# A small store of 444-byte rows moved from among the last loads to behind them

## The chip, the cores and the metric

The kernel runs on one core of one Trainium2 chip. The metric is device time in microseconds (us) of one execution. Lower is better. The executions of this kernel agree within about 0.3%.

## The reference

The input is x of 32 x 512 x 1024 float32. Negative values become zero, and the last axis is summed:

```python
def reference(x):
    relu_x = np.maximum(x, 0)
    return np.sum(relu_x, axis=-1).astype(np.float32)
```

That is 67.11 MB to read and 64 KB to write.

## The kernel before

SP issues every transfer in program order. Seven large pieces of x go through three buffers. Then comes a tail of ever smaller loads, down to three pieces of one last row per partition (512, 224 and 288 columns). ACT and DVE share the compute. The 128 results of a partition leave in three stores: 128 results that were transposed first (four runs of 128 bytes, "the four-run store"), 111 results per partition (128 rows of 444 bytes, "the 444-byte store"), and the 16 results of the tail (64 bytes per partition, "the last store"). SP's end of the program, shortened:

```python
    # ... tail loads: rows of 8, 4, 2, 1 per partition, then the last row in three pieces
    for k, (lo, hi) in enumerate([(0, n0), (n0, n1), (n1, D)]):
        sp.dma_start(out=parts[k], in_=xv[-1][:, BIG - 1, lo:hi]).then_inc(
            s_in[NBIG + len(TAIL) + k] if k < 2 else s_part, 16
        )
    sp.wait_ge(s_fact, 1)          # the last results of the 444-byte store are there
    sp.wait_ge(s_fdve, 1)
    sp.dma_start(out=ov[1][:, :], in_=res[:, start[1] : start[2]]).then_inc(s_store, 16)
    sp.wait_ge(s_turn, 1)
    sp.dma_start(
        out=of[0:P].rearrange("(k q) -> k q", q=32), in_=turned[0:P:32, 0:32]
    ).then_inc(s_store, 16)
    # ...
    sp.wait_ge(s_tdve, 1)          # the very last result
    sp.dma_start(out=ov[-1][:, :], in_=res[:, start[-1] : J]).then_inc(s_out, 16)
    sp.wait_ge(s_store, 16 * (len(REGIONS) - 1))
    sp.wait_ge(s_out, 16)
```

The compute of the last row matters too. Note that one semaphore, `s_part`, counts the last load (16) and the two engines (1 each):

```python
    act.wait_ge(s_in[-2], 16)
    on_act(parts[0], last[:, n : n + 1]).then_inc(s_part, 1)
    dve.wait_ge(s_in[-1], 16)
    on_dve(parts[1], last[:, n + 1 : n + 2]).then_inc(s_part, 1)
    dve.wait_ge(s_part, 16 + 2)
    on_dve(last[:, :], res[:, J - 1 : J]).then_inc(s_tdve, 1)
```

## Time and profile before

| | before |
|---|---|
| median of 3 runs | 161.09 us (160.91 to 161.38) |
| profiled execution | 161.31 us, span 160.0 us |
| DVE, ACT busy | 76%, 63% of the span |
| DMA queue of SP | 97.8% of 16 engines' span, 420 GB/s |
| chain that ended last | loads 68%, ACT 18%, DVE 11%, SP 1% |

The kernel is bound by its loads, and after them by a short end of compute and one store. A number of the chain is the share of the span in which that piece of work was what the end waited for.

### The profile page before, as it was taken

To read this page: it belongs to the slowest core of one execution; us is meant where nothing else is said; L and a number is where in the kernel's file an instruction comes from. 1 tells how busy PE (TensorE), PEld (TensorE's weight loads), DVE (VectorE), ACT (ScalarE), POOL (GpSimd) and SP (SyncE) were. 2 spreads that over 40 slices of the span, in tenths; PEclk is the share of its full clock that TensorE was granted. 3 is DMA by queue.
4 is the path that set the end of the run, shared out by engine and by line. 5 is a ranking of instruction groups with operands and counts; after the bars stand their busy time and mean duration, and the time that the engine had idled before them with its cause. 6 is when DMAs were issued, how large, how long until landed. Compare 5 with 4: busy or idle time off the path is not lost.

```text
span 160.0 us, 150 instructions
## 1 busy us (share of the span) xinstructions
DVE 121.6 (76%) x59; ACT 101.4 (63%) x55; POOL 0.2 (0%) x4
## 2 busy tenths in 40 slices
DVE  0000000999959999999979989699899999598994
ACT  3000059990799708996099942999339980596973
POOL 0000000000000000000000000000000000000000
DMA  9997996996996997997998979969969969999993
GB/s 377 492 399 338 492 524 262 524 524 262 524 508 279 524 475 311 524 442 344 524 410 377 524 344 443 524 295 492 524 295 492 524 262 524 393 393 406 418 387 119
DMA packets 2457, 67.18 MB, mean 420 GB/s; under 512 B 536, under 2 KB 792, under 8 KB 1176
## 3 DMA queue, kind: packets, MB, share of 16 engines
q1 hardware_dynamic: 2456, 67.18, 97.8%
q14 instruction: 1, 0.01, 0.0%
HBM read 67.11 MB, written 0.07 MB: 420 GB/s over the span
## 4 chain that ended last, share of the span: by engine, by line
DMA 68%; ACT 18%; DVE 11%; SPq 1%; issue 0%
DMA buf<-in_x_dram 68%; ACT buf L137 18%; DVE res L152 11%; ACT buf L119 1%; SPq L98 1%; DVE last L122 0%
## 5 line engine op out<-in xcount | busy, mean ns | idle before, releaser
L152 DVE TENSOR_REDUCE res<-buf 128x7 f32<-128x7168 f32 (+4 forms) x17 | 100.1, 5920 | 33.6 <-ACT buf L137 33.6
L137 ACT ACTIVATE buf<-buf 128x7168 f32<-128x7168 f32 (+4 forms) x16 | 80.7, 5099 | 45.9 <-DMA buf<-in_x_dram 45.9
L119 ACT ACTIVATE buf<-buf 128x1024 f32<-128x1024 f32 (+1 forms) x19 | 19.0, 1001 | 9.2 <-DMA buf<-in_x_dram 9.2
L122 DVE TENSOR_SCALAR_CACHE_REDUCE buf<-buf 128x1024 f32<-128x1024 f32 (+2 forms) x19 | 20.8, 1144 | 2.9 <-DMA buf<-in_x_dram 2.7
L119 ACT ACTIVATION_READ_ACCUMULATOR buf<-buf 128x1 f32 x19 | 3.6, 187 | 0.0
L137 ACT ACT_TABLE_LOAD x1 | 1.3, 1283 | 1.3 <-PEq L215 1.3
L122 DVE DVE_READ_ACCUMULATOR buf<-buf 128x1 f32 x19 | 1.6, 82 | 0.0
L122 DVE TENSOR_SCALAR_CACHE_REDUCE last<-last 128x290 f32<-128x290 f32 x1 | 0.5, 455 | 0.2 <-ACT buf L119 0.2
L161 DVE STREAM_TRANSPOSE turned<-res 128x32 f32<-128x32 f32 x1 | 0.2, 211 | 0.0
L185 DVE TENSOR_TENSOR res<-half 128x1 f32<-128x1 f32 x1 | 0.2, 160 | 0.1
L215 POOL MEMSET const-bfloat16-1.0<- 128x1 bf16 x1 | 0.1, 101 | 0.0
L215 POOL MEMSET const-uint8-127<- 128x1 uint8 x1 | 0.1, 101 | 0.0
L215 POOL MEMSET const-float32-0.0<- 128x1 f32 x1 | 0.1, 98 | 0.2 <-issue 0.2
L215 POOL MEMSET const-float32-1.0<- 128x1 f32 x1 | 0.1, 98 | 0.0
L122 DVE DVE_READ_ACCUMULATOR last<-last 128x1 f32 x1 | 0.1, 82 | 0.0
## 6 DMA issues: line engine op xcount, KB each, us to landing
buf<-in_x_dram SPq DMA_DIRECT2D x1, 7680.0 KB, 21.3
buf<-in_x_dram SPq DMA_DIRECT2D x1, 4096.0 KB, 26.7
buf<-in_x_dram SPq DMA_DIRECT2D x1, 2048.0 KB, 31.2
buf<-in_x_dram SPq DMA_DIRECT2D x2, 512.0 KB, 18.8
buf<-in_x_dram SPq DMA_DIRECT2D x1, 1024.0 KB, 33.2
buf<-in_x_dram SPq DMA_DIRECT2D x1, 256.0 KB, 34.4
last<-in_x_dram SPq DMA_DIRECT2D x1, 144.0 KB, 34.3
buf<-in_x_dram SPq DMA_DIRECT2D x1, 112.0 KB, 34.1
```

Source lines behind the costliest of these rows:

```text
L98: sp.dma_start(out=buf[:, tb, r : r + n, :], in_=xv[-1][:, r : r + n, :]).then_inc(s_in[NBIG + i], 16)
L119: return act.activation(t, t, AF.Relu, accum_out=acc)
L122: return dve.tensor_scalar(out=t, in0=t, scalar1=0.0, scalar2=None, op0=ALU.max, op1=ALU.add, accum_out=acc)
L137: act.activation(t, t, AF.Relu).then_inc(s_act, 1)
L152: dve.tensor_reduce(out=res[:, c * BIG + r : c * BIG + r + n], in_=buf[:, c % NB, r : r + n, :], axis=X, op=ALU.add,).then_inc(s_dve, 1)
L161: dve.transpose(out=turned[:, :], in_=res[:, 0:32]).then_inc(s_turn, 1)
L185: dve.tensor_tensor(out=res[:, j0 + r : j0 + r + 1], in0=half[:, 0:1], in1=half[:, 1:2], op=ALU.add)
L215: nc = _bacc.Bacc("TRN2", target_bir_lowering=False, num_devices=1)
```

## The change

The intent: the small writes of the 444-byte store are suspected of disturbing the loads beside which they run, so that store waits until the last load but one has landed. The four-run store, which takes SP longest to issue (0.63 us), goes ahead of it so that it is out of the way.

```diff
-    sp.wait_ge(s_fact, 1)
-    sp.wait_ge(s_fdve, 1)
-    sp.dma_start(out=ov[1][:, :], in_=res[:, start[1] : start[2]]).then_inc(s_store, 16)
     sp.wait_ge(s_turn, 1)
     sp.dma_start(
         out=of[0:P].rearrange("(k q) -> k q", q=32), in_=turned[0:P:32, 0:32]
     ).then_inc(s_store, 16)
+    sp.wait_ge(s_fact, 1)
+    sp.wait_ge(s_fdve, 1)
+    sp.wait_ge(s_in[-1], 16)
+    sp.dma_start(out=ov[1][:, :], in_=res[:, start[1] : start[2]]).then_inc(s_store, 16)
```

## The prediction

> **What bounds the kernel now.** I began with the page's chain of work that ended last, because the change touches only the last microseconds of the program and only what is on that chain there can move the time.
>
> ```profile
> DMA 68%; ACT 18%; DVE 11%; SPq 1%; issue 0%
> DMA buf<-in_x_dram 68%; ACT buf L137 18%; DVE res L152 11%; ACT buf L119 1%; SPq L98 1%; DVE last L122 0%
> ```
>
> No store stands on it. The loads of x carry 68% of the span; the rest is two earlier rounds of compute that release buffers, the issue of the tail loads, and a short end. The chain in order of time shows that end (start, duration, what):
>
> ```profile
> 122.21 34.19 DMA buf<-in_x_dram
> 156.40 0.02 issue
> 156.42 1.56 ACT buf L119 x4
> 157.98 0.02 issue
> 158.00 0.46 DVE last L122 x2
> ```
>
> The reader is to see where the chain leaves the loads: at 156.40, with the landing of the last whole row (the load issued at 122.21). From there ACT is the bound, with half of that row and then half of the last row back to back, 1.56 us, then one DVE instruction, 0.46 us, and then the last store. Loads that land after 156.40 (the three pieces of the last row) do not set the end: ACT is not idle between its two pieces, and the DVE's last instruction waits for ACT, not for a DMA:
>
> ```profile
> 157.08 0.63 ACT L119 ACTIVATE buf<-buf 128x512 f32<-128x512 f32 x1
> 158.00 0.46 DVE L122 TENSOR_SCALAR_CACHE_REDUCE last<-last 128x290 f32<-128x290 f32 x1 [0.24 <-ACT buf L119]
> ```
>
> Next I asked for SP's own order of issues, since SP issues every transfer of this kernel in program order:
>
> ```profile
> 147.17 0.35 SPq L111 DMA_DIRECT2D out_dram<-res  x1
> 147.56 0.63 SPq L113 DMA_DIRECT2D out_dram<-turned  x1
> 158.49 0.34 SPq L199 DMA_DIRECT2D out_dram<-res  x1
> ```
>
> L111 is the store of 128 rows of 444 bytes (111 results per partition), L113 the four-run store, L199 the last store (16 results, 64 bytes, per partition). The first two go out at 147, when ten microseconds of loads are still to come. It looks as if they disturb those loads. The stretches of the tail say otherwise (columns: stretch, length, DVE, ACT and POOL busy, clock, DMA share, GB/s):
>
> ```profile
> 146.50:156.25 9.75, 8.82 (x16) 7.61 (x14) 0.00 (x0) 1.00 0.98 401
> 156.25:156.75 0.50, 0.33 (x1) 0.33 (x1) 0.00 (x0) 1.00 1.05 369
> 156.75:157.25 0.50, 0.44 (x3) 0.50 (x3) 0.00 (x0) 1.00 0.91 289
> 157.25:157.50 0.25, 0.21 (x2) 0.25 (x1) 0.00 (x0) 1.00 0.18 49
> 157.50:159.25 1.75, 0.73 (x4) 0.30 (x2) 0.00 (x0) 1.00 0.00 0
> 159.25:159.50 0.25, 0.00 (x0) 0.00 (x0) 0.00 (x0) 1.00 0.36 32
> ```
>
> Two things are to be seen: the engines are full until 156.75 and then run empty, and from 157.50 until the last store starts at about 159.3 they do nothing at all, a hole of 1.75 us. The packets of the trace by size say whose these are: the first 444-byte packet starts at 156.84 and the last ends at 157.54, although their store was issued at 147.17. They waited 9.7 us behind the loads. The last pieces' load packets run until 157.36, so 0.5 us of the store lies beside the end of the loads, on engines that have finished their own.
>
> **What the Trainium skill says.** (1) "DMA: Bandwidth & Descriptors", section "Queues, rings and completion order": on each DMA engine the descriptors of one issuing queue are consumed in ring order. The trace agrees: issued at 147.17, first packet 156.84, when the first engine runs out of loads. (2) The same page, "Specifications": below 512 bytes a transfer does a read-modify-write, so 444-byte rows are presumably what made the author suspicious. The trace shows 25 ns for a 444-byte packet against 41 ns for 896 bytes and 51 ns for 1,152, that is 56, 46 and 44 ps per byte: a quarter dearer per byte, not a multiple. (3) "Perfetto Trace Analysis", section "DMA Instruction — HWDGE (DVE, Sync)": the final semaphore write waits for the data to be written, which can take surprisingly long towards HBM. This trace shows no such delay for these stores: the last 64-byte packet starts at 159.52, the last semaphore write 159.53, and the execution ends at 160.0.
>
> **The change, part by part.** The instructions and their number are the same on every engine; the listing of SP's order shows two DMA issues swapped and one wait added (for the 224-column piece, the last load but one).
>
> (a) *The four-run store moves ahead.* It waits only for the transpose after the second round, long done when SP has issued its loads at 123.69 + 0.44 = 124.1. It is then issued at about 124.2 instead of 147.56. SP has nothing else to do there (the next wait is for the compute until 147.17), so its 0.63 us is free. Its four packets took 13 ns each; still issued after all loads, they still queue behind them. Effect on the path: 0.
>
> (b) *The 444-byte store stays away from the loads.* It moves from 147.17 to the landing of the 224-column piece. The last 896-byte packet ends at 156.98, its last semaphore write at about 157.00, so issue at about 157.05. The last store gives the time from issue to first packet: 158.49 to 159.33, 0.84 us. So packets from 157.9. Each engine has 128/16 = 8 rows, at some 21 to 25 ns each 0.2 us (the trace shows them spaced 21 ns): done by about 158.1. This is inside the idle hole from 157.50 to 159.3.
>
> (c) *What is gained.* The most the store could have cost the loads is its own engine time, 128 x 25 ns / 16 engines = 0.2 us, 0.12% of the time, and only if it lay ahead of them. It did not. On the engines that finish last, the 1,152-byte packets are spaced 47 ns while the store runs beside them and 47 ns before it began: no slowing to recover. And the chain left the loads at 156.40, before the first 444-byte packet at 156.84. Gain on the path: 0.0 us.
>
> (d) *What is lost.* SP is busy with this issue from 157.05 to 157.40 and must be free at 158.49 for the last store: 1.1 us to spare. If the wait ended only when the DVE took up the piece, at 157.37, SP would be free at 157.72 and the packets done by 158.5: still before 159.3. The last two waits of the program (stores done) see the earlier store done at least 0.8 us before the last one. Loss on the path: 0.0 us.
>
> Sum: 0.0. From the median of 161.09, and with the slight leaning towards a gain that a quieter end of the loads might have, I say 161.05.
>
> **The rivals.** *First, contention:* the small writes slow the last loads, by sharing memory rather than an engine, and taking them away brings landings forward. For it: in 156.75 to 157.25 the rate falls to 289 GB/s while the DMA share is 0.91. Against it: short packets alone explain that, the packet spacing did not change, and only landings after 156.40 could profit, for which nobody on the chain waits. Even granting all 0.2 us the time would be 160.9. *Second, a new late completion:* the 444-byte store is now so late that its completion ends the program, or its issue holds up the last store on SP. For it: the distance falls from 1.8 us (157.54 to 159.33) to about 1.2 us, and a write receipt of some 2 us, which the skill's delay in (3) would allow, would end near 160. Against it: no receipt shows in this trace. It would make 161.3 to 161.6. *Third, the early four-run store gets in front:* if its packets at 124 ran at once, they would cost four packets of 13 ns among loads, nothing that can be measured. *Fourth, the last store starts later*, because descriptors of the 444-byte store still fill its queue: it would need them to be unfinished at 159.3, 1.2 us later than computed; if so, 161.3.
>
> **Range and chances.** The three runs of before span 160.91 to 161.38, 0.3%. My effect is between -0.2 (first rival in full) and +0.4 (second rival), most likely within 0.05 of nothing, so the scatter of the runs sets the range: 160.70 to 161.45. A gain of over 2% would need 3.2 us; the whole end after the loads' leg of the chain is 160.0 - 156.4 = 3.6 us and the change removes none of it. A loss of 2% would need the store to finish at about 163. I give 0.01 to faster, 0.98 to within 2%, 0.01 to slower.
>
> **What would show each step right or wrong.** Right: the four-run store's issue near 124.2; the 444-byte store's issue between 157.0 and 157.4; packets under 512 bytes gone from 157.0 to 157.4 but for semaphore writes, and a burst near 157.9 to 158.2 in the former hole; the chain still leaving the loads near 156.4, ACT 1.56 us, DVE 0.46 us and the last store's issue 2.1 us after the loads' leg; no store on the chain but the last. Wrong: a chain whose last load leg ends more than 0.1 us earlier relative to the start of the tail loads (contention was real), a final issue that follows another SP issue directly, or a span that ends with the 444-byte store's landing. A shift of the whole program by some tenths, with the end from 156.4 on unchanged, would be scatter and say nothing of the change.

## More of the kernel before

The three calls of experiments ran on three chips (7, 15 and 2, four kernels each), so times are compared within a call. All runs told of are with a granted clock of 1.00. Where "the trace's records" are named, they are the packet and semaphore records from which the profile is made.

## The result

| | median | runs | range |
|---|---|---|---|
| before | 161.06 us | 6 | 160.91 to 161.38 |
| changed | 160.98 us | 6 | 160.84 to 161.12 |

The ratio is 0.9993, with a 95% interval of 0.998 to 1.0006: the same. Ratios are the mean time of one kernel's runs over that of the other's of the same rounds, so they are not quite the ratio of the medians quoted.

SP's issues in the changed kernel, in order of time (start, duration, line, what):

```profile
123.50 0.44 SPq L106 DMA_DIRECT2D last<-in_x_dram  x1
123.99 0.63 SPq L110 DMA_DIRECT2D out_dram<-turned  x1
157.16 0.34 SPq L116 DMA_DIRECT2D out_dram<-res  x1
158.05 0.34 SPq L200 DMA_DIRECT2D out_dram<-res  x1
```

The four-run store goes out at 123.99, directly behind the loads, and the 444-byte store at 157.16, as predicted. The packets of the 444-byte store are now in the hole that the DMA engines had near the end. The stretches of the changed kernel (columns as in the prediction: stretch, length, DVE, ACT and POOL busy, clock, DMA share, GB/s):

```profile
157.25:157.50 0.25, 0.23 (x2) 0.25 (x2) 0.00 (x0) 1.00 0.00 0
157.50:157.75 0.25, 0.19 (x1) 0.03 (x1) 0.00 (x0) 1.00 0.00 0
157.75:158.50 0.75, 0.27 (x2) 0.00 (x0) 0.00 (x0) 1.00 0.27 76
158.50:158.75 0.25, 0.00 (x0) 0.00 (x0) 0.00 (x0) 1.00 0.00 0
158.75:159.25 0.50, 0.00 (x0) 0.00 (x0) 0.00 (x0) 1.00 0.19 17
```

The work of 157.75 to 158.50 is the 444-byte store (the trace's records: first packet 158.00, last 158.32), and the last store follows from 158.88.

The chain that ended last, in the changed kernel, in order of time:

```profile
122.06 34.02 DMA buf<-in_x_dram
156.09 0.02 issue
156.11 1.43 ACT buf L120 x4
157.53 0.02 issue
157.56 0.46 DVE last L123 x2
```

It has the same pieces as before, but the load's leg is 0.17 us shorter than before (34.19) and ACT's leg 0.13 us shorter (1.56), although ACT has the same four instructions with the same durations. I had not predicted the second. With another 0.14 us from the start of the tail loads, which lies before the change takes effect and so is scatter, this makes up the 0.44 us by which the two profiled spans differ (159.953 and 159.510 in the trace's records). The medians, however, differ by 0.08 us only. Either the profiled execution of before was unlucky, or it shows something that most executions hide. That question set the experiments.

The shorter ACT leg has this explanation in the trace's semaphore records. The DVE's last instruction waits for `s_part` to reach 18. Before, ACT's increment came at 157.81, but the last of the sixteen increments of the last load came at 157.98, and the instruction began at 158.00. In the changed kernel the load's last came at 157.40, ACT's at 157.53, and the DVE began at 157.56. So the line that my prediction quoted, "0.24 <-ACT buf L119", named the wrong releaser. One semaphore with several writers does not tell the profile who came last.

### The profile page after: what moved, and what is told of

The parts are those of the page before. It is cut to its first block, busy times and chain, and to the rows that moved or that the text cites. A ratio compares the mean times of both kernels' runs of the same rounds, so it can differ in the third digit from the quotient of the medians. Undisturbed runs are those within 1.5% of the kernel's fastest.

```text
span 159.5 us, 150 instructions
## 1 busy us (share of the span) xinstructions
DVE 121.6 (76%) x59; ACT 101.5 (64%) x55; POOL 0.2 (0%) x4
## 4 chain that ended last, share of the span: by engine, by line
DMA 68%; ACT 18%; DVE 11%; SPq 1%; issue 0%
DMA buf<-in_x_dram 68%; ACT buf L138 18%; DVE res L153 11%; ACT buf L120 1%; SPq L98 1%; DVE last L123 0%
```

## The experiments

Twelve kernels ran. Theory Q is my prediction's: the early store queues behind the loads and takes nothing from the path. Its rivals grew with the results; each theory is explained in the expectation that first names it. All results were correct but that of the kernel that leaves a store out on purpose. "Completion lag" is, by the trace's records, the time from the end of the last packet of the last load (1,152-byte packets) to the last of that load's sixteen semaphore increments. "Gap" is from ACT's end to the start of the DVE's last instruction.

| kernel | median us (range) | before, same call | ratio (95% interval) | profiled us | completion lag | gap |
|---|---|---|---|---|---|---|
| before (first profile) | 161.09 | | | 161.31 | 0.62 | 0.20 |
| changed | 160.98 (160.84 to 161.12) | 161.06 | 0.9993 (0.998 to 1.0006) | 160.86 | 0.45 | 0.03 |
| e_after_again | 160.90 (160.85 to 161.02) | 160.94 | 0.9998 (0.9985 to 1.0012) | 160.85 | 0.45 | 0.03 |
| e_no_store | 160.90 (160.86 to 160.99) | 160.94 | 0.9997 (0.9985 to 1.001) | 160.90 | 0.45 | 0.03 |
| e_early_x8 | 163.24 (163.10 to 163.50) | 160.94 | 1.0144 (1.013 to 1.0157) | 163.12 | 0.31 | 0.03 |
| e_wait_only | 162.19 (162.08 to 162.34) | 160.94 | 1.0076 (1.0063 to 1.0088) | 162.21 | 0.45 | 0.03 |
| e_before_again | 161.14 (160.98 to 161.48) | 161.05 | 1.0006 (0.9992 to 1.002) | 161.48 | 1.07 | 0.54 |
| e_split_before | 161.07 (160.96 to 161.42) | 161.05 | 1.0001 (0.9988 to 1.0013) | 161.11 | 0.62 | 0.13 |
| e_late_four | 161.10 (160.87 to 161.37) | 161.05 | 1.0000 (0.9987 to 1.0013) | 161.26 | 0.66 | 0.13 |
| e_just_before_last | 162.28 (162.24 to 162.34) | 161.05 | 1.0073 (1.006 to 1.0086) | 162.34 | 0.43 | 0.03 |
| e_swap_only | 161.14 (160.97 to 161.47) | 160.96 | 1.0011 (0.9998 to 1.0023) | 161.47 | 1.07 | 0.52 |
| e_split_after | 160.98 (160.91 to 161.12) | 160.96 | 1.0002 (0.999 to 1.0015) | 161.12 | 0.47 | 0.13 |
| e_act_queue | 161.24 (160.97 to 161.44) | 160.96 | 1.0022 (1.0008 to 1.0036) | 160.97 | 0.45 | 0.03 |
| e_wait_last | 161.25 (160.97 to 161.41) | 160.96 | 1.0014 (1.0002 to 1.0027) | 161.41 | 0.45 | 0.13 |

### e_after_again: the changed kernel once more

No edit. 

> The changed kernel again, beside the kernel before on one chip, to narrow the interval. Theory Q (the early store queues behind the loads and takes nothing from the path): ratio 1.000, within 0.0005 of it, 161.06 us. Rival C (the store's packets hold up the completion of the last load, whose last semaphore increment came at 157.98 in the trace before, 0.17 us after ACT's; in the trace after ACT was last by 0.14 us): 0.1 to 0.2 us faster, ratio 0.9988 to 0.9994.

It came out at 160.90 beside 160.94. The effect, 0.04 us, is nearer to Q than to C, and zero effect (a ratio of 1) is within the interval. The profile repeats the first one's: lag 0.45, gap 0.03.

### e_no_store: what the store costs at all

Against the changed kernel:

```diff
-    sp.wait_ge(s_fact, 1)
-    sp.wait_ge(s_fdve, 1)
-    sp.wait_ge(s_in[-1], 16)
-    sp.dma_start(out=ov[1][:, :], in_=res[:, start[1] : start[2]]).then_inc(s_store, 16)
...
-    sp.wait_ge(s_store, 16 * (len(REGIONS) - 1))
+    sp.wait_ge(s_store, 16)
```

> The changed kernel with the 444-byte store left out (14,208 results are not written: the result is wrong on purpose). It shows all that this store can cost wherever it stands. Theory Q: as the changed kernel and as the kernel before, within 0.1 us. Rival C: as the changed kernel, and 0.1 to 0.2 us faster than before. Rival L (the late store costs something at the end): faster than the changed kernel by 0.1 us or more.

160.90 us, just as the changed kernel's 160.90 of the same call. In the changed kernel the store is hidden as far as these runs can tell, so Rival L is out. Against the kernel before, all that could be gained is of the order of 0.05 us in the median.

### e_early_x8: the early store eight times over

```diff
     sp.dma_start(out=ov[1][:, :], in_=res[:, start[1] : start[2]]).then_inc(s_store, 16)
+    for i in range(7):
+        sp.dma_start(out=spare[i], in_=res[:, start[1] : start[2]]).then_inc(s_store, 16)
```

(with `spare` an internal tensor in HBM, and the last wait raised by 7 x 16.)

> The kernel before with the early 444-byte store made eight times (seven copies into a spare tensor), all issued from 147.2 us on. 64 packets per DMA engine instead of 8, some 1.4 us, from 156.8 to 158.3 and on the slowest engine from 157.3 to 158.7: still before the last store's packets at 159.3. Theory Q: same time as before within 0.15 us, and the last load's completion no later against its packets than before. Rival C: the hold-up grows with the number of packets, at least 0.3 us slower, the DVE's last instruction waiting longer after ACT's end.

It took 163.24 us, 2.3 us more. Q is out for eight stores; C had said "at least 0.3 us slower", but by another way than the one that the trace shows. The last three lines of its chain, and the issue of its last store with that store's time to landing (last column, us), are:

```profile
157.29 0.73 ACT buf L122 x2
158.02 0.02 issue
158.05 0.46 DVE last L125 x2
```

```profile
out_dram<-res SPq DMA_DIRECT2D x1, 8.0 KB, 3.2
```

The DVE is released by ACT, with a gap of 0.03, so the last load's completion was not held up and the cost did not come where Rival C wanted it. It came behind: the last store landed 3.2 us after its issue instead of 1.4 us. By the records the 1,024 packets of 444 bytes ran from 157.14 to 159.86 and took 33 ns each in the mean (the longest 234 ns) instead of the 25 ns of one store's, and the completions of the eight stores went on until 161.54, 1.7 us after the last of these packets. This pile of writes was completed at one 57 KB store per 0.47 us or so (128 increments from 157.74 to 161.54, eight stores in 3.8 us), and the last store's own last increment came at 161.72, behind them. The loads were late as well: the last 1,152-byte packet ended 36.86 us after the first tail load's issue, against 36.16 to 36.25 in eleven of the other profiles (the first of before has 36.48, e_act_queue 36.35). What made them late no run tells.

### e_wait_only: the wait without the swap

```diff
     sp.wait_ge(s_fact, 1)
     sp.wait_ge(s_fdve, 1)
+    sp.wait_ge(s_in[-1], 16)
     sp.dma_start(out=ov[1][:, :], in_=res[:, start[1] : start[2]]).then_inc(s_store, 16)
```

> The added wait alone, without the swap: the 444-byte store issues at about 157.1, the four-run store (0.63 us on SP) behind it at about 157.5, so SP is free only at about 158.1 to 158.2, where the changed kernel issued its last store at 158.05. Theory Q: 0.1 us slower than the changed kernel (161.1 against 161.0), the last store's issue directly behind the four-run store's. If the swap is worth nothing: the same time as the changed kernel within 0.03 us.

I had expected 0.1 us and found 1.29 us over the changed kernel of the same call. SP's issues in this kernel:

```profile
157.28 0.35 SPq L112 DMA_DIRECT2D out_dram<-res  x1
157.68 0.63 SPq L114 DMA_DIRECT2D out_dram<-turned  x1
158.36 0.39 SPq L200 DMA_DIRECT2D out_dram<-res  x1
```

The last store's issue does follow the four-run store's directly, 0.31 us later than in the changed kernel. But the DVE's last instruction, too, started 0.12 us later in this profile (157.68 and 157.56), so about 0.2 us is SP's. The other 1.0 us is in the store's landing:

```profile
out_dram<-res SPq DMA_DIRECT2D x1, 8.0 KB, 2.4
```

By the records fifteen of its sixteen increments were there at 159.84, and the last came at 160.80. The swap is thus no ornament: without it the added wait is a clear loss of 0.76%.

### e_before_again: a second profile of before

No edit. 

> The kernel before, unaltered, for a second profile of it. The first profile was of a run of 161.31 us, 0.25 over its median. Question: are its late pieces (the last 1,152-byte packet 36.48 us after the first tail load's issue, against 36.19 to 36.21 in the four profiles without an early store; the last load's completion 0.17 us after ACT's last) the early store's doing or that run's scatter? Theory Q (scatter): 36.2 and ACT last, as in the changed kernel. Rival C (contention): 36.4 to 36.5 again and the load last. Ratio to before 1.000 by construction.

The packets are those of the other kernels (the last ends 36.23 us after the first tail load's issue), so the late packets of the first profile were scatter. The late completion came again, 1.07 us after that packet, and ACT's leg of the chain shows the wait:

```profile
156.18 0.02 issue
156.21 1.92 ACT buf L119 x4
158.13 0.02 issue
```

The view lays the wait to ACT, 1.92 us for the four instructions that take 1.43 us in the changed kernel. By the records ACT's increment came at 157.62 and the load's last at 158.13.

### e_split_before: a semaphore of its own for the last load

```diff
-            s_in[NBIG + len(TAIL) + k] if k < 2 else s_part, 16
+            s_in[NBIG + len(TAIL) + k] if k < 2 else s_pload, 16
...
-    dve.wait_ge(s_part, 16 + 2)
+    dve.wait_ge(s_pload, 16)
+    dve.wait_ge(s_part, 2)
```

> The kernel before with the semaphore of the DVE's last wait split in two: one for the last load, one for ACT and DVE, so that the profile can tell who released it. Same time as before within 0.1 us. Theory Q: the DVE's last instruction waits for ACT, as my prediction read it. Rival C: it waits for the DMA into last, by 0.1 to 0.2 us, as the semaphore records of the first profile have it.

The view of who waited for whom, in us:

```profile
DVE last L123 <- DMA last<-in_x_dram: 0.2, 1, 0.2
```

With its own semaphore the load is named as the releaser. It came 0.03 us after ACT's part here, so this execution lost next to nothing. The 0.13 us gap is mostly the split's own: its partners e_split_after and e_wait_last have the same.

### e_late_four: the four-run store held back alone

```diff
+    sp.wait_ge(s_in[-1], 16)
     sp.wait_ge(s_turn, 1)
     sp.dma_start(
         out=of[0:P].rearrange("(k q) -> k q", q=32), in_=turned[0:P:32, 0:32]
```

> The kernel before, with the 444-byte store early as it was, and the four-run store alone held back to the landing of the 224-column piece. It is issued at about 157.2, done on SP at 157.85, before the last store's turn at about 158.1. It tells apart two causes of the 1.25 us that the added wait without the swap cost, of which only 0.3 us are SP's lateness and 1.0 us is one of sixteen completions of the last store coming late. Theory F (the four-run store's few writes just ahead of the last store's on the same engines hold that completion up): the last store's landing grows from 1.4 to about 2.4 us, the time by about 0.8 to 1.0 us over before. Theory B (the pile of both stores' writes does it): landing stays near 1.4 us and the time within 0.15 us of before.

The last store landed 1.4 us after its issue, and the time is 161.10 beside 161.05. Theory F is out: a late four-run store by itself does no harm. The completion lag is 0.66 here, with the 444-byte store early.

### e_just_before_last: how late is too late

Against the changed kernel:

```diff
-    sp.wait_ge(s_fact, 1)
-    sp.wait_ge(s_fdve, 1)
-    sp.wait_ge(s_in[-1], 16)
-    sp.dma_start(out=ov[1][:, :], in_=res[:, start[1] : start[2]]).then_inc(s_store, 16)
...
     sp.wait_ge(s_tdve, 1)
+    sp.wait_ge(s_fact, 1)
+    sp.wait_ge(s_fdve, 1)
+    sp.dma_start(out=ov[1][:, :], in_=res[:, start[1] : start[2]]).then_inc(s_store, 16)
```

> The changed kernel with the 444-byte store held back further, until the last result is there, so that it is issued directly ahead of the last store. How late is too late? SP's issue alone delays the last store by 0.39 us. Theory Q as I wrote it (no receipt, packets alone): 0.4 us slower than the changed kernel, landing of the last store 1.4 us. Theory B (HBM writes complete slowly after their packets, about 0.66 us for the 444-byte store in the trace after, and later writes queue behind): 0.7 to 1.5 us slower, landing of the last store 1.8 us or more.

162.28 us beside 161.05, 1.2 us slower, with the last store landing after 2.4 us. Issue order on SP explains 0.39 us of it and the landing 1.0 us (less 0.1 to 0.2 that before has and this has not). Again one of sixteen increments is the late one (160.94, the fifteenth 160.44). That is what Theory B said; Q as written falls.

### e_swap_only: the swap without the wait

```diff
-    sp.wait_ge(s_in[-1], 16)
```

(taken from the changed kernel.) 

> The swap alone, without the added wait: four-run store at about 124, 444-byte store at 147.2 as before. Theory C2 (an early 444-byte store makes the completion of the last load late: so far 0.62 to 1.07 us after its last packet in four profiles with the early store, 0.43 to 0.45 in five without): the last load's completion at least 0.55 us after its last packet, and the time that of the kernel before, 0.05 to 0.1 us over the changed kernel. Theory D (it is the four-run store that follows the 444-byte one early that does it): 0.45 us and the changed kernel's time. Theory Q: no difference of any kind.

The lag is 1.07: fifteen of the last load's increments were there at 157.41, the sixteenth came at 158.13, and ACT had been done at 157.64. This profile is as Theory C2 has it, and D is out, since the four-run store is far away here. The time was 161.14 beside 160.96, on the side of C2 but with 1.000 at the edge of the interval (0.9998).

### e_split_after: the partner of the split

The same edit as e_split_before, on the changed kernel. 

> The changed kernel with the semaphore of the DVE's last wait split, the partner of the same split of the kernel before, where the DVE's last instruction waited 0.2 us for the DMA into last. Theory C2: here it is released by ACT (or by nothing that the profile shows), not by that DMA, and the time is 0.05 to 0.1 us under the split kernel before (161.07). Theory Q: the same releaser in both.

```profile
DVE last L124 <- ACT buf L121: 0.2, 1, 0.2
```

Here ACT releases the DVE, as C2 says. The time, 160.98, is 0.09 us under e_split_before's, but each is level with its own call's before (ratios 1.0002 and 1.0001), so this pair shows no gain in time.

### e_act_queue: the early store on the other queue

```diff
-    sp.wait_ge(s_fact, 1)
-    sp.wait_ge(s_fdve, 1)
-    sp.dma_start(out=ov[1][:, :], in_=res[:, start[1] : start[2]]).then_inc(s_store, 16)
...
+    act.wait_ge(s_fact, 1)
+    act.wait_ge(s_fdve, 1)
+    act.dma_start(out=ov[1][:, :], in_=res[:, start[1] : start[2]]).then_inc(s_store, 16)
     for r, n, s in tail[:-1]:
```

> The kernel before with the 444-byte store issued on ACT's queue instead of SP's, at the same moment, 147.2. It tests whether the queue order is what kept the early store behind the loads. If so, its packets now go at once, at about 148, among the loads, and are complete by 150: no store near the end, the last load's completion 0.45 us after its last packet as in the changed kernel; the loads behind it come later by its 0.2 us of engine time at most. Time between the changed kernel's 160.9 and 161.2. If the packets still come only at 156.8, the order is not a matter of the queue.

Packets of 150.50 to 153.75 us in this kernel, and then in the kernel before:

```profile
DMA packets 290, 1.30 MB, mean 401 GB/s; under 512 B 158, under 2 KB 158, under 8 KB 158
```

```profile
DMA packets 150, 1.29 MB, mean 396 GB/s; under 512 B 16, under 2 KB 16, under 8 KB 16
```

The 128 rows now run in the midst of the loads (records: 150.60 to 153.63), not at 156.8, so it was the queue that had kept them back. They were later than I had said, 3.6 us after the issue at 147.02, and no run tells why. The completion lag is 0.45, as wherever no early store shares the loads' queue. But the loads pay: the last packet ends 36.35 us after the first tail load's issue, about 0.15 us later than in the changed kernel, near the 0.2 us of engine time that the prediction worked out. The time is 161.24 beside 160.96. That is slower (1.0022, interval above 1), a little beyond the 161.2 that I had allowed. The profiled run, 160.97, doesn't show this, and the loads explain only part of it: in the four unprofiled runs the time exceeds the core's span by 1.50 to 1.64 us, in every other run of this document by 1.31 to 1.41. So some 0.2 us lies outside the span in which the program's instructions run, and no run tells what it is.

### e_wait_last: one load later

```diff
-    sp.wait_ge(s_in[-1], 16)
+    sp.wait_ge(s_pload, 16)
```

(on e_split_after.) 

> The changed kernel with split semaphores, and the 444-byte store waiting for the last load instead of the last but one: issue at about 157.5 instead of 157.16, done on SP at 157.85, 0.2 us before the last store's turn. The completions of the store then fall at about 158.9 to 159.3, across the last store's first packets at 158.9, without the two issues being back to back. It tells apart two causes of the late completion of the last store in the runs with the wait alone and with the store just ahead of the last. Theory W (writes of an earlier store still outstanding): landing of the last store over 1.6 us, the time 0.2 to 0.9 us over the changed kernel. Theory S (issues back to back on SP): landing 1.4 us, the changed kernel's time within 0.1 us.

SP's issues, and the last store's landing:

```profile
157.55 0.35 SPq L117 DMA_DIRECT2D out_dram<-res  x1
158.18 0.34 SPq L202 DMA_DIRECT2D out_dram<-res  x1
```

```profile
out_dram<-res SPq DMA_DIRECT2D x1, 8.0 KB, 1.8
```

There are 0.28 us between the issues and still the landing grew to 1.8 us and the median by 0.27 us over e_split_after (161.25 and 160.98, same call). By the records the 444-byte store's last increment came at 159.82, 1.1 us after its last packet, and the last store's increments, which follow its packets of 159.02 to 159.23, only at 159.43 to 159.99. Theory W fits, and S (issues back to back) is not needed. One load later seems already too late, though the times of the two kernels overlap (160.97 to 161.41, and 160.91 to 161.12).

## Why the prediction was right or wrong

The verdict and the range were right: 160.98 us inside 160.70 to 161.45, and the same within 2%. By its steps:

**Where the kernel is bound, and the queueing of the early store: right.** The load's leg, ACT's four instructions, the DVE's last instruction and the last store are the end in every profile. e_act_queue shows that the queue kept the early store back: on the other queue the same store, issued at the same time, ran about four to six microseconds earlier, and the loads ended about 0.15 us later.

**Step (a), the four-run store: right, and underrated.** Its issue moved to 123.99 and cost nothing there. But I gave the swap a value of 0.0, and it is what makes the wait harmless: without it the wait costs 1.29 us, of which about 0.2 us is SP's time and about 1.0 us the last store's landing.

**Step (b), the place in the hole: right, in part by luck.** Issue at 157.16 (predicted 157.05), packets from 158.00 to 158.32 (predicted 157.9 to 158.1). But 157.05 came of a misreading: I took the semaphore packet at 157.00 for the landing of the 224-column piece, whose last increment came at 157.345 in that trace. In the changed kernel the landing was 0.51 us after that piece's last packet (157.07 and 156.56), and the issue fell near my figure because this packet ended 0.42 us earlier than in the first profile of before. My alternative, 157.37, was what that trace bore out.

**Step (c), "Gain on the path: 0.0 us": wrong for the profiled executions, and nearly right for the medians.** What failed is the claim that no load after 156.40 is waited for. In the first pair even one of my signs of being wrong came up: the load's leg ended 35.35 us after the start of the tail loads instead of 35.52, which I had said would mean contention. But e_before_again, the same kernel as before, has 35.35 too, so that was scatter. The packets of the loads were indeed not slowed (36.20 to 36.25 us after the first tail load's issue in four profiles of the five with one early store on SP's queue). But the DVE waits until the last load's semaphore is complete, and that I had not looked at. With one early 444-byte store in the same queue the lag was 0.62, 1.07, 0.62, 0.66 and 1.07 us in five profiles. In the eight without it (changed, e_after_again, e_split_after, e_no_store, e_wait_only, e_just_before_last, e_wait_last, e_act_queue) it was 0.43 to 0.47 us. The difference stands within each of the two later calls too (0.62 to 1.07 against 0.43, and 1.07 against 0.45 to 0.47), so it is not one of chips. The late completion held the DVE's last instruction back by 0.1 to 0.5 us after ACT's release in four of those five. The eightfold store does not fit: it was early and in the same queue, and its lag was 0.31.

In unprofiled runs most of it is not seen: the medians differ by 0.04 to 0.08 us. At first sight the slow runs agree with it: of 58 runs with one early 444-byte store on SP's queue (all runs of before with e_before_again, e_split_before, e_late_four and e_swap_only) 11 took over 161.2 us. Of 21 runs without it and without a penalty of another kind (changed, e_after_again, e_split_after, e_no_store) none did, the highest being 161.12. But nine of the eleven fell in one call (that of e_before_again, e_split_before and e_late_four, 29 such runs on one chip), in which none of the 21 was run; in the other calls it is 2 of 29 against 0 of 21. So whether the change takes away an occasional delay, or that chip was the less steady one, is not shown. What holds the late increment back is open as well. Profiling may itself contribute, since from the changed kernel on every profiled execution is a first run.

**Step (d), "Loss on the path: 0.0 us": right for this kernel, with a margin that was mis-sized.** I reckoned with packets and took the store for done at 158.1, or 158.5 if issued at 157.37, "still before 159.3". Its sixteen completions came at 158.55 to 158.99, and the last store's packets began at 158.88. This overlap of 0.1 us did no harm (e_split_after has the same), but there was little room left: e_wait_last, with the issue at 157.55, lost 0.27 us, and e_just_before_last 1.2 us. The term missing from the sum is the time from the store's last packet to its last increment: 0.66 us here, 0.44 and 0.73 us in e_after_again and e_split_after. I missed it because I took the last semaphore packet (159.53 in the trace of before) for the completion of the last store; its increments came at 159.73 to 159.91. The 2 us that my second rival took for a receipt (the confirmation that a write has landed) were an assumption, from no number of the trace. But this rival, which I had set aside because "no receipt shows in this trace", was right in kind: what comes late is a completion, and only the changed kernel's timing kept it out. The fourth, a last store that starts later, shows in part: in e_wait_only and e_just_before_last its first packet came 0.88 and 0.92 us after its issue instead of 0.83, and its packets then ran for 0.63 and 0.55 us instead of 0.2.

**Which version is best?** None beat the changed kernel: e_no_store, without the 444-byte store, takes the same 160.90 us. Moving this store further has nothing left to win that these runs could show. Nor is the changed kernel shown to be faster than before.

## What to carry to other kernels

In this kernel a store issued early on the queue of the loads was held back by that queue, so moving it behind them won next to nothing. What matters at the end is when semaphores are complete, which came 0.4 to 1.1 us after the last packet here (with one 444-byte store) and has to be read from its own records. A late store should be complete, not merely sent, when the last store of the program begins (an overlap of 0.1 us did no harm, one of 0.8 us did), and where SP issues several stores the slow issue belongs before the wait. When several producers share a semaphore, give the suspected one its own before believing what the view says of who released the wait.

## What the Trainium skill lacked or had wrong

- "Perfetto Trace Analysis", section "DMA Instruction — HWDGE (DVE, Sync)", says that the last semaphore write can come surprisingly late, above all when HBM is the target, and gives no number there; the breakdown of a fixed cost that the skill has elsewhere is for transfers issued from GpSimd. These runs have numbers for SP: 0.43 to 0.47 us from a load's last packet to its last increment when nothing is near, 0.62 to 1.07 us with one 444-byte store behind it in the same queue (a load, so SBUF is the target), and 0.44 to 0.73 us for the 444-byte store itself in the changed kernel and its split. My prediction took the semaphore packet for the completion and so called the delay absent.
- "DMA: Bandwidth & Descriptors", section "Latency and other measured facts", gives about 0.6 us to the first byte for a transfer issued by SP, without saying from where it counts. Here it was 0.83 to 0.84 us from the start of the issue to the first packet (158.05 to 158.88 and 157.16 to 158.00 in the changed kernel).
- The same page, "Specifications", says that under 512 bytes a transfer does a read-modify-write, without its cost. Packets of 444 bytes took 25 ns each in one store, and 33 ns in the mean in a pile of eight, whose completions came at one 57 KB store per 0.47 us.
- "DMA: Bandwidth & Descriptors", section "Queues, rings and completion order", does say that a semaphore increment lands only after every earlier write of its DMA engine, which fits the late landings here, but no page says how much a small store loses by it: the last store's landing grew from 1.4 us to 1.8, 2.4 and 3.2 us, in two of these kernels through one increment out of sixteen.
